# A hybrid encoder trunk on one core: two Strassen products moved between quarters, other preparation of the latents' weights

## The chip, the cores and the metric

The kernel runs on one core of a Trainium2 chip. The metric is the device time of one execution in microseconds, the median of several runs. The core has TensorE (matmuls, PE in the profile), VectorE (DVE), ScalarE (ACT), GpSimd (POOL) and SyncE (SP, which here only issues DMAs). Each engine works through its own instructions in order and waits on semaphores for the others.

## The reference

The input is a sequence of 512 tokens with 1024 channels, in float32, and everything stays float32 in effect. There are two layers, each a mixer and a feed-forward part, with an RMS norm before and after each:

```python
k_nope, k_rope, v = mla_shared_kv(h, ...)      # once, after layer 0
# layer 0's mixer: conformer_conv; layer 1's mixer: mla_attention on the shared K and V
h = h + rms_norm(m, mix_post_g[layer])
f = jnp.square(jax.nn.relu(rms_norm(h, ffn_pre_g[layer]) @ w_ff1[layer])) @ w_ff2[layer]
h = h + rms_norm(f, ffn_post_g[layer])
```

`mla_shared_kv` makes a latent of 256 for keys and values (`dkv`) with an RMS norm of its own, and a rotary key (`kr`). `mla_attention` makes a latent of 384 for the queries (`dq`), normalises it, and projects it to 8 heads of 128 plain and 64 rotary dimensions. Scores are scaled by 192 to the power −0.5, masked by chunks, and go through a softmax. The feed-forward part goes from 1024 to 4096 and back.

## The kernel before

**Splits.** A float32 matmul is made of three matmuls in a rounded type (`F32R`). Each operand is split into a high part (a ScalarE copy that rounds) and a low part (VectorE: operand minus high part), and the kernel adds high·high, high·low and low·high. Weights are split on the chip too: `weight(key)` loads a 128 x 1024 block into a `raw` tile and writes `wh` and `wl` tiles; there are 5 of each. For some blocks (`lo_by_dma`) ScalarE writes minus the high part instead, and an accumulating DMA of GpSimd's queue adds the weights. The latents' blocks `dq`, `dkv` and `kr` are first multiplied by a norm's gain, in eight GpSimd operations per block (`TENSOR_SCALAR raw<-raw,vt`), then split that way.

**Feed-forward.** `feed_forward(layer, X, F)` works in four quarters of the 4096 inner channels. In each, eight ff1 blocks of 24 matmuls give squared activations `Z`, and the second matrix is multiplied by Strassen's scheme over halves of tokens, of inner channels and of output columns: seven products of 24 matmuls. For each, `terms(p)` builds the left operand (a difference of two `Z` halves, then the split: four tiles per product), `weight` the right one (a sum or difference of blocks), and `collect` adds the two PSUM results to accumulators on VectorE. The order is `(3, 6, 2, 1, 4, 5, 7)` in quarters 0 to 2 and `(3, 5, 1, 4, 7, 2, 6)` in the last, so that there the first half of the tokens (blocks 0 and 1) is finished by products 5 and 7, and products 2 and 6 (`TOGETHER`) close the second half, one token block at a time. After the third quarter the accumulators are combined into the four output quadrants.

**Norm behind it.** `post_norm` takes the finished half rows. `residual` squares them (ScalarE, with a sum) and multiplies by the gain; `rms` and `rsqrt_tiny` make the scale in some ten VectorE operations of one or two columns (tiles `stat`), and `add_norm` adds the result to the residual `h`. In layer 0 it does so by halves of the tokens (`HA`, `HB`) and `prenorm` then transposes `h` on TensorE into 16 tiles `XH`. In layer 1 it does so by single blocks, with the gain's product on VectorE or GpSimd (`VG`), and each block is stored.

**Latents.** For each half, `latent("dq", ...)`, `latent("dkv", ...)` and the rotary key are made: products with `XH`, squares added, a sum over channels on TensorE, `rsqrt_tiny`, the scale spread over the partitions by four matmuls, then scaling, splitting and reordering. The projections of the first heads follow, and the attention, head by head: scores, `TENSOR_TENSOR_REDUCE` with the mask (it appears as `CUSTOM_DVE_ANT_0`), exponential with a sum on ScalarE, reciprocal and product on VectorE, transposes, and the product with the values.

**Tiles.** 50 tiles `big` of 128 x 512, 6 `tmp`, 6 `mm` and 2 `bc` in PSUM, and 8 `stat` serve everything.

**The order of work** is made by a planner in the program. It records all operations, gives each a due time from the recorded order of the matmuls, and plays the engines with costs (`cost`) and latencies; every engine takes the ready operation with the earliest due time, TensorE the one recorded first. DMAs are issued at most 16 us (`LEAD`) ahead. A `big` tile is given to an operation only when more tiles are free than tiles recorded earlier still wait for one. [...] Short matmuls with the identity (cost `FILL`) are put into planned gaps of TensorE. All instructions are issued through one helper, so the profile has them all on line 630, and one goes by tile names.

## Time and profile before

| | |
|---|---|
| median of 3 runs | 1086.79 us (1085.52 to 1087.72) |
| profiled execution, its own time | 1087.92 us |
| its span, first to last instruction | 1086.1 us |
| mean granted TensorE clock | 0.987 |
| HBM read, written | 197.58 MB, 5.51 MB |
| instructions | 15288 |

A name such as `wl<-raw,wh` is output from inputs. `mm<-big,wh` of 512 columns is an ff1 product or a projection, `mm<-wh,big` of 512 columns a Strassen product, `mm<-big,wh` of 256 columns a latent's product. A group's row has its count, its busy time and the mean time of one in ns, and then the idle time in front of it with what ended it. Consecutive instructions of one engine overlap in these records, so that an operation's duration is longer than the step from one to the next. The stages: convolution until about 205 us, layer 0's feed-forward until about 540, latents and attention until about 730, layer 1's feed-forward until 1069.7.

### The profile page before, as it was taken

The numbers are of one execution on the slowest core, as the hardware profiler recorded it, in microseconds if no ns is written. First come the engines' busy times: TensorE is split into PE (matmuls) and PEld (weight loads), VectorE is DVE, ScalarE is ACT, GpSimd is POOL, SyncE is SP. The second block draws the span as 40 slices with busy tenths as digits, with TensorE's granted clock in tenths as the row PEclk, the third lists the DMA queues.
The fourth block names the chain that finished last, engine by engine and source line by source line (L and its number), as shares of the span: only waits on it lengthen the run. The fifth ranks groups of instructions, "written<-read, shape, count | busy, mean of one in ns | idle before, by whom it ended". The sixth has DMA issues, their size and how long they took to land.

```text
span 1086.1 us, 15288 instructions
## 1 busy us (share of the span) xinstructions
PE 1046.9 (96%) x5310; PEld 889.3 (82%) x5310; DVE 762.1 (70%) x1523; ACT 643.5 (59%) x1364; POOL 191.1 (18%) x227
## 2 busy tenths in 40 slices
PE   9999989999999999999798999999999999999993
PEld 7888978988888888888687888889888888878883
DVE  6599973856458559848877977456663584588598
ACT  8563586956555455456775876568665644544561
POOL 1110011101001001002953443211010010010022
PEclk9999999999999999999899999999999999999997
DMA  8998687768958858839652133348596597588682
GB/s 271 315 282 222 206 232 194 175 162 241 236 144 239 237 143 238 259 122 265 158 138 74 50 97 120 135 157 210 153 256 201 153 245 216 156 216 228 197 213 78
DMA packets 67614, 207.25 MB, mean 191 GB/s; under 512 B 7632, under 2 KB 13904, under 8 KB 67536
## 3 DMA queue, kind: packets, MB, share of 16 engines
q1 hardware_dynamic: 48960, 150.16, 40.8%
q0 software_dynamic: 14400, 52.44, 26.7%
q10 hardware_dynamic: 4176, 3.67, 1.1%
q8 instruction: 42, 0.69, 0.3%
q14 instruction: 36, 0.29, 0.1%
HBM read 197.58 MB, written 5.51 MB: 187 GB/s over the span
## 4 chain that ended last, share of the span: by engine, by line
PE 78%; DVE 8%; DMA 6%; ACT 4%; issue 2%; POOL 2%; DVEq 0%; SPq 0%; POOLq 0%; ACTq 0%
PE mm L630 75%; DMA raw<-wts 4%; DVE big L630 4%; PE bc L630 3%; DVE wl L630 2%; ACT big L630 2%; DVE stat L630 2%; POOL raw L630 2%; ACT wh L630 1%; DMA wl<-raw 1%; DMA wl<-wts 1%; ACT wl L630 1%; DVE tmp L630 0%; DVE h L630 0%; DMA big<-xT 0%
## 5 line engine op out<-in xcount | busy, mean ns | idle before, releaser
L630 PE MATMUL mm<-big,wh 128*128 128x512 f32 (+1 forms) x1704 | 476.9, 364 | 2.0 <-ACT wh L630 0.8
L630 PE MATMUL mm<-wh,big 128*128 128x512 f32 (+1 forms) x1216 | 374.2, 387 | 5.7 <-ACT wh L630 2.9
L630 PEld LDWEIGHTS mm<-big,wh 128*128 128x128 f32 x1704 | 307.2, 190 | 52.6 <-DVE big L630 1.5
L630 ACT ACTIVATE wh<-raw 128x512 fp32r<-128x512 f32 (+2 forms) x456 | 258.8, 612 | 135.0 <-DMA raw<-wts 67.1
L630 DVE TENSOR_TENSOR wl<-raw,wh 128x512 fp32r<-128x512 f32 (+1 forms) x353 | 230.1, 689 | 145.0 <-ACT wh L630 144.5
L630 PE MATMUL mm<-big,wl 128*128 128x512 f32 (+1 forms) x852 | 309.4, 364 | 2.9 <-DMA wl<-raw 2.0
L630 PEld LDWEIGHTS mm<-wh,big 128*128 128x128 f32 x1216 | 227.1, 189 | 51.7 <-ACT wh L630 3.7
L630 PE MATMUL mm<-wl,big 128*128 128x512 f32 (+1 forms) x608 | 234.4, 387 | 2.6 <-DVE wl L630 2.6
L630 PEld LDWEIGHTS mm<-big,wl 128*128 128x128 f32 x852 | 161.4, 190 | 28.1 <-DMA wl<-raw 2.2
L630 POOL DMA_DIRECT2D raw<-wts x64 | 55.3, 864 | 557.2 <-DVE big L630 181.8
L630 PEld LDWEIGHTS mm<-wl,big 128*128 128x128 f32 x608 | 114.7, 189 | 27.4 <-DVE wl L630 5.0
L630 ACT ACTIVATE tmp<-mm 128x512 f32<-128x512 f32 (+1 forms) x72 | 39.8, 553 | 118.0 <-PE mm L630 118.0
L630 ACT ACTIVATE big<-tmp 128x256 f32<-128x256 f32 (+1 forms) x208 | 96.3, 494 | 21.1 <-DVE tmp L630 19.6
L630 DVE TENSOR_TENSOR big<-big,big 128x512 f32<-128x512 f32 (+5 forms) x101 | 69.5, 705 | 16.8 <-ACT big L630 16.1
L630 ACT ACTIVATE big<-mm 128x512 f32<-128x512 f32 (+5 forms) x110 | 57.5, 527 | 30.7 <-PE mm L630 29.9
L630 DVE TENSOR_TENSOR tmp<-big,big 128x512 f32<-128x512 f32 x80 | 53.7, 684 | 28.8 <-ACT big L630 28.7
L630 DVE TENSOR_TENSOR big<-big,mm 128x512 f32<-128x512 f32 x104 | 67.6, 677 | 4.6 <-PE mm L630 4.4
L630 DVE TENSOR_TENSOR big<-tmp,big 128x512 fp32r<-128x512 f32 (+1 forms) x93 | 59.7, 648 | 15.6 <-ACT big L630 13.6
L630 DVE SCALAR_TENSOR_TENSOR big<-big,vt,big 128x512 fp32r<-128x512 f32 (+20 forms) x95 | 63.2, 730 | 6.0 <-ACT big L630 6.0
L630 POOL DMA_DIRECT2D wl<-wts x30 | 26.5, 882 | 183.6 <-ACT wl L630 137.2
L630 ACT ACTIVATE wl<-raw 128x512 fp32r<-128x512 f32 x72 | 42.1, 623 | 13.2 <-POOL raw L630 6.1
L630 PE MATMUL mm<-big,big 128*128 128x512 f32 (+3 forms) x256 | 45.7, 325 | 0.0
(85 smaller groups left out, 810.9 us busy)
## 6 DMA issues: line engine op xcount, KB each, us to landing
raw<-wts SPq DMA_DIRECT2D x228, 512.0 KB, 5.1
raw<-wts POOLq DMA_DIRECT2D x64, 512.0 KB, 7.6
wl<-wts POOLq DMA_DIRECT2D x30, 512.0 KB, 8.4
big<-cw SPq DMA_DIRECT2D x45, 256.0 KB, 7.0
wl<-raw POOLq DMA_DIRECT2D x6, 512.0 KB, 5.2
row<-along SPq DMA_DIRECT2D x5, 512.0 KB, 4.5
raw<-wts SPq DMA_DIRECT2D x12, 192.0 KB, 2.4
big<-xT SPq DMA_DIRECT2D x8, 256.0 KB, 5.2
```

The source lines that it names most:

```text
L630: return f(*args, **kwargs)
```

## The change

- In both layers, products 2 and 6 of the third quarter are no longer made there. Their left operands are built at the end of that quarter and kept; the products are made in the fourth quarter behind product 7, into the PSUM tiles to which the fourth quarter's products 2 and 6 then add. Their four collecting sums go. The orders are now `(3, 6, 2, 1, 4, 5, 7)`, the same, `(3, 1, 4, 5, 7)` and `(3, 5, 1, 4, 7)`, the fourth followed by 2 and 6 of both quarters.
- The latents' blocks go into `big` tiles (`scaled`): two raw, two high and two low tiles per block, the gain by one VectorE product per 512 columns, the low part by VectorE. GpSimd's scalings and accumulating DMAs for them go.
- The queries' latent is not normalised. It is split straight from PSUM with `q_norm_g` as scale (`query_latent`), and the scale per query, together with 192 to the power −0.5, is kept in `wq` and applied in the softmax: one more VectorE operation per score tile, and a scale per row in the exponential. The order per half is now `dkv`, `kr`, `dq` 0 and 1; `dq` 2 is made once, for all tokens.
[...]
- The gain's product of the last norm stays on VectorE (`GAIN_ON`); `post_norm` takes its groups of blocks as an argument (`PAIRS`, `SINGLES`, `by_halves`), with the same groups as before.

The diff, cut to this:

```diff
-PRODUCTS = (3, 6, 2, 1, 4, 5, 7), (3, 5, 1, 4, 7, 2, 6)
+PRODUCTS = ((3, 6, 2, 1, 4, 5, 7),) * 2 + ((3, 1, 4, 5, 7), (3, 5, 1, 4, 7))
...
-        for p in PRODUCTS[q == 3]:
+        for r, p in [(q, p) for p in PRODUCTS[q]] + [(r, p) for r in (2, 3) for p in TOGETHER if q == 3]:
...
-FILL = 216.0
+FILL = 222.0
...
-            wide = [a for a in aps[1] if a.tensor.space != PSUM and _size(a) > 8]
+            wide = [a for a in aps[1] if a.tensor.space != PSUM]
...
+    def scaled(name, src):
+        lo, hi = ([big(F32R) for _ in range(2)] for _ in range(2))
+        for o in range(2):
+            raw = big()
+            nc.sync.dma_start(out=raw, in_=src[:, o * T : (o + 1) * T])
+            g0 = VEC[GAINS[name[0]]] + 4 * o
+            gain = vt[:, g0 : g0 + 4].rearrange("p (k o) -> p k o", o=1).to_broadcast([P, 4, P])
+            nc.vector.tensor_tensor(
+                out=raw.rearrange("p (k m) -> p k m", m=P), in0=raw.rearrange("p (k m) -> p k m", m=P), in1=gain, op=ALU.mult
+            )
+            split(raw, slice(0, T), (hi[o], lo[o]))
+        return hi, lo
...
-                    nc.gpsimd.tensor_scalar(
-                        out=raw[:, ks], in0=raw[:, ks], scalar1=v(GAINS[name[0]], k), scalar2=None, op0=ALU.mult
-                    )
...
+            steps = [(u, i) for u in range(2) for i in range(2)]
+            for p in PRODUCTS[q]:
+                A = terms(p)
+                collect(p, product({}, A, sides(q, p), steps))
...
+            if q > 1:
+                for p in TOGETHER:
+                    both[q, p] = terms(p)
             if q == 3:
-                both = {p: terms(p) for p in TOGETHER}
+                pts = {p: product({}, both[2, p], sides(2, p), steps, last=False) for p in TOGETHER}
+                w = {p: sides(3, p) for p in TOGETHER}
                 for i in range(2):
                     for p in TOGETHER:
-                        collect(p, product(*both[p], [(0, i), (1, i)]))
+                        product(pts[p], both[3, p], w[p], [(0, i), (1, i)], first=False)
+                        collect(p, {i: pts[p][i]})
                         yield done((1, int(p == 6)), i)
...
-            residual(F, g, b, dh, 16 + 2 * (b % nb) + dh, st[i], VG if nb == 1 else GAIN_ON, r2)
+            residual(F, g, b, dh, 16 + 2 * (b - bs[0]) + dh, st[bs], GAIN_ON, r2)
...
+    def query_latent(m, t):
+        t0, n = t
+        pt = products(("dq", m), XH, t0, n)
+        src, nat = dealt_part(pt[:, :n]), slice(t0, t0 + n)
+        hi, lo = (undealt(a, t) for a in CQ[m])
+        nc.scalar.activation(hi, src, AF.Copy, scale=v("q_g", m))
+        nc.vector.scalar_tensor_tensor(
+            out=lo, in0=src, scalar=v("q_g", m), in1=hi.bitcast(F32), op0=ALU.mult, op1=ALU.subtract
+        )
...
-        latent("dq", "q_g", CQ, t, 384)
...
+        for m in range(2):
+            query_latent(m, t)
+    query_latent(2, FULL)
...
+    nc.vector.tensor_copy(out=r, in_=sums([(b, r1n, b) for b in range(TB)], 0, D))
+    sm = sums([(b, qsq, b) for b in range(TB)], 0, 384)
...
+    nc.vector.scalar_tensor_tensor(out=wq, in0=y, scalar=8.0 * scale, in1=r, op0=ALU.mult, op1=ALU.mult)
...
-                out=S[:, ks], in0=sc[:, ks], in1=mask[:, T - nkey :], scale=-scale, scalar=-NEG,
-                op0=ALU.add, op1=ALU.min, accum_out=st[:, 0:1],
+                out=S[:, ks], in0=sc[:, ks], in1=mask[:, T - nkey :], scale=1.0, scalar=NEG,
+                op0=ALU.add, op1=ALU.max, accum_out=st[:, 0:1],
             )
-            nc.scalar.activation(S[:, ks], S[:, ks], AF.Exp, scale=-1.0, bias=st[:, 0:1], accum_out=st[:, 2:3])
+            w = wq[:, i : i + 1]
+            nc.vector.tensor_scalar(out=st[:, 1:2], in0=st[:, 0:1], scalar1=w, scalar2=-1.0, op0=ALU.mult, op1=ALU.mult)
+            nc.scalar.activation(S[:, ks], S[:, ks], AF.Exp, scale=w, bias=st[:, 1:2], accum_out=st[:, 2:3])
```

## The prediction

> **What bounds the kernel now.** I read the page first (sections 1, 2 and 4), then the windows around the two places that the change touches, then TensorE's waits and the timelines there.

> ```profile
> span 1086.1 us, 15288 instructions
> PE 1046.9 (96%) x5310; PEld 889.3 (82%) x5310; DVE 762.1 (70%) x1523; ACT 643.5 (59%) x1364; POOL 191.1 (18%) x227
> PE 78%; DVE 8%; DMA 6%; ACT 4%; issue 2%; POOL 2%; DVEq 0%; SPq 0%; POOLq 0%; ACTq 0%
> ```

> TensorE is the bound nearly everywhere, and the change takes away almost no matmul. So it can only fill stretches in which TensorE stands. Stage by stage (columns: window, length, busy PE, PEld, DVE, ACT, POOL, granted clock, DMA share, GB/s):

> ```profile
> 435.00:489.60 54.60, 54.60 (x243) 45.21 (x242) 36.24 (x60) 26.78 (x54) 2.59 (x3) 1.00 0.64 191
> 489.60:516.80 27.20, 27.20 (x122) 22.52 (x121) 23.95 (x40) 16.03 (x32) 8.80 (x13) 1.00 1.00 262
> 516.80:559.40 42.60, 34.73 (x201) 29.97 (x200) 33.31 (x90) 31.82 (x79) 37.87 (x52) 0.88 0.69 163
> 516.80:606.00 89.20, 78.45 (x507) 70.27 (x506) 68.94 (x186) 63.89 (x153) 54.10 (x69) 0.94 0.47 116
> 522.50:525.90 3.40, 2.92 (x9) 1.90 (x7) 3.40 (x6) 3.40 (x7) 2.48 (x3) 0.50 0.89 175
> 606.00:727.00 121.00, 119.36 (x667) 103.22 (x667) 81.04 (x208) 78.51 (x186) 40.13 (x34) 1.00 0.37 121
> 950.00:990.00 40.00, 38.51 (x168) 30.98 (x167) 35.75 (x61) 18.73 (x35) 3.45 (x4) 1.00 0.84 230
> 1031.30:1058.60 27.30, 27.30 (x122) 22.59 (x121) 26.37 (x45) 17.68 (x35) 6.68 (x6) 1.00 0.88 216
> 1058.60:1069.70 11.10, 11.07 (x49) 8.75 (x47) 11.03 (x24) 3.52 (x10) 2.54 (x2) 1.00 0.00 0
> 1069.70:1082.70 13.00, 0.00 (x0) 0.00 (x0) 12.97 (x42) 1.79 (x6) 3.94 (x3) 0.59 0.31 115
> ```

> A 512-column matmul costs 54.60/243 = 0.225 us, a Strassen product of 24 costs 5.4 us. Five products of layer 0's last quarter end at 516.8, and layer 1's at 1058.6. Two places are slack. From 516.8 to 606 (products 2 and 6, the latents, the first projections) TensorE is idle 89.20 − 78.45 = 10.7 us, and the clock is 0.12 × 42.6 = 5.1 us short in three half-rate stretches, one of which is shown: 15.8 us recoverable. And after the last matmul VectorE alone works for 13.0 us. What TensorE waits for from 516.8 to 606 (total, times, longest), and the worst case of it:

> ```profile
> PE mm L630 <- ACT wh L630: 2.9, 1, 2.9
> PE mm L630 <- DVE big L630: 2.5, 2, 2.3
> PE bc L630 <- DVE stat L630: 2.0, 2, 1.6
> PE mm L630 <- DMA wl<-raw: 2.0, 1, 2.0
> 534.24 0.63 ACT L630 ACTIVATE wl<-raw 128x512 fp32r<-128x512 f32 x1 [1.25 <-POOL raw L630]
> 535.39 1.13 ACT L630 ACTIVATE wh<-raw 128x512 fp32r<-128x512 f32 x2
> 536.05 1.19 PE L630 MATMUL mm<-wh,big 128*128 128x512 f32 x2 [2.90 <-ACT wh L630]
> L630 POOL TENSOR_SCALAR raw<-raw,vt 128x128 f32<-128x128 f32 x48 | 35.6, 972 | 2.3 <-DMA raw<-wts 2.3
> wl<-raw POOLq DMA_DIRECT2D x6, 512.0 KB, 5.2
> ```

> ScalarE runs in order. The latents' `wl<-raw` waits there for GpSimd's gain, and behind it stands the `wh<-raw` that product 6 needs. So GpSimd's 48 scalings (35.6 us) hold TensorE twice: through ScalarE, and through the accumulating DMA behind them (5.2 us). The 2.0 us for `stat` are the normalisations of the latents.

> **The change part by part.** Prices: VectorE's 128x512 operation repeats every (2.47 − 0.68)/3 = 0.60 us.

> ```profile
> 500.09 2.47 DVE L630 TENSOR_TENSOR big<-big,mm 128x512 f32<-128x512 f32 x4
> L630 DVE TENSOR_TENSOR wl<-raw,wh 128x512 fp32r<-128x512 f32 x5 | 3.2, 680 | 0.0
> L630 DVE SCALAR_TENSOR_TENSOR big<-big,vt,tmp 128x256 f32<-128x256 f32 x10 | 4.5, 478 | 2.8 <-ACT tmp L630 2.7
> L630 DVE TENSOR_TENSOR big<-big,big 128x256 fp32r<-128x256 f32 x10 | 7.0, 731 | 0.8 <-ACT big L630 0.7
> L630 DVE TENSOR_TENSOR big<-big,tmp 128x256 f32<-128x256 f32 x5 | 2.6, 529 | 0.9 <-ACT tmp L630 0.8
> 560.71 0.16 DVE L630 TENSOR_TENSOR stat<-bc,stat 128x2 f32<-128x2 f32 x1 [0.75 <-PE bc L630]
> 562.68 0.16 DVE L630 TENSOR_TENSOR stat<-stat,stat 128x2 f32<-128x2 f32 x1
> big<-cw SPq DMA_DIRECT2D x45, 256.0 KB, 7.0
> ```

> The chain of 11 small operations (first and last row) takes 562.84 − 560.71 = 2.1 us.

> *Latents' weights and the moved products, 516.8 to 606.* Removed: 48 GpSimd scalings, 12 ScalarE copies, 6 accumulating DMAs. Added on VectorE: per block two gain products and two low parts, 6 × 4 × 0.60 = 14.4 us; on SP, 12 loads of 256 KB in place of 6 of 512 KB, which now wait for big tiles. The queries' normalisation goes from the chain: 2 × (3 × 0.478 + 3 × 0.731 + 2 × 0.529 + 2.1) = 13.6 us of VectorE. In its place come four half and one full-width scaled low part (6 half widths × 0.73 = 4.4), squares added (4 half widths, 2.9), and one chain for `wq` (2.5): 9.8 us, off the path, because 39 matmuls of projections (8.8 us) stand ahead of the first softmax; without that cover the 2.5 us of the `wq` chain would be a wait. The postponed products bring eight low parts of weights into the quarter, 4.8 us, half of them ahead of 516.8. VectorE there: 68.9 + 14.4 − 13.6 + 9.8 + 2.4 = 82 us. TensorE: 78.45 − 5.1 of slow clock + 48 × 0.225 = 84.2 us, entered 10.8 us earlier. Perfectly packed this gains 15.8 us. VectorE at 97% would be as full as from 1031.3 to 1058.6 (26.37 of 27.30), where TensorE did not wait at all; from 516.8 on, though, norms in chains alternate with matmuls. Bounds: 0 (VectorE's order makes as many waits as GpSimd's did; below it lies the rival on tiles) and 15.8. I take 8, half: the waits by GpSimd (2.9 + 2.0), and half of clock and rest.

> The half-rate stretches follow waits of 2.0 to 2.9 us, and each costs 1.7 us. [...]

> *The tail of layer 1.* VectorE after 1058.6:

> ```profile
> L630 DVE SCALAR_TENSOR_TENSOR stat<-stat 128x1 f32<-128x1 f32 x20 | 5.8, 308 | 0.0
> L630 DVE TENSOR_TENSOR stat<-stat 128x1 f32<-128x1 f32 x12 | 2.6, 227 | 0.0
> L630 DVE SCALAR_TENSOR_TENSOR stat<-stat,r 128x1 f32<-128x1 f32 x4 | 1.7, 419 | 0.0
> L630 DVE TENSOR_SCALAR stat<-stat 128x1 int32<-128x1 int32 x4 | 0.6, 148 | 0.0
> L630 DVE SCALAR_TENSOR_TENSOR h<-big,stat,h 128x512 f32<-128x512 f32 x8 | 5.7, 744 | 0.0
> L630 POOL TENSOR_TENSOR big<-big,row 128x512 f32<-128x512 f32 x7 | 9.8, 1404 | 23.0 <-ACT tmp L630 23.0
> ```

> It works 11.03 + 12.97 = 24.0 us past product 7. Of that 20 × 0.16 + 12 × 0.08 + 4 × 0.27 = 5.2 us are stretched small operations (0.15 us is the undisturbed price), while GpSimd multiplies by the gain: five of its seven products fall here (x2 and x3 in the windows). In the changed kernel these five go to VectorE, 3.0 us, and the stretching goes; (2,6)'s low parts add 2.4 to 4.8. That is 24 to 27 us, against 2 × 5.4 + 11.1 = 21.9 us of matmuls behind product 7, so VectorE's backlog at the last matmul falls from 13 to about 2 to 5 us. Then the last block's own chain decides: collecting sum 0.7, square 0.6 like the ScalarE copies above, small chain 2.1, two sums 1.4, and signals between them: about 5.5. I put 8 us in place of 13: −5. Bounds: 0 and −7.5.

> [...]

> *Attention.* One more small VectorE operation per score tile, 32 in all, between maximum and exponential, and a scale from memory on the exponential.

> ```profile
> L630 DVE RECIPROCAL stat<-stat 128x1 f32<-128x1 f32 x32 | 4.9, 157 | 3.0 <-ACT big L630 2.8
> PE bc L630 <- DVE big L630: 1.1, 2, 0.8
> ```

> Priced as the reciprocal that it resembles, 4.9 us of VectorE at 67% load; from 606 to 727 TensorE waits 1.1 us for it. Bounds −0.5 and +5; I take +0.8, near the wait, since the next head's scores cover it.

> *Smaller parts.* The third quarter loses two products with their weights and four collecting sums, with less VectorE work per matmul; product 1, which subtracts weights, moves up to second place. The 950 to 990 window shows 1.5 us idle there; −1.5 to +2, taken as 0. The eight operand tiles kept until the fourth quarter take 8 of 50 big tiles; free ones while ff1 runs cover it. `dq` 2 at full width is 24 matmuls for 48 of half the width: 0. The planner's new costs reorder everything slightly: ±2, taken as 0.

> Sum: −8 − 5 + 0.8 = −12.2 us. The profiled execution took 1087.92 us (span 1086.1): 1087.9 − 12.2 = 1075.7. It stands 1.1 above the runs' median of 1086.79, from which the same sum gives 1074.6; I put 1075.

> **The rivals.**

> *Everything hidden.* Transition and tail both reach their bounds: 1087.9 − 15.8 − 7.5 + 0.8 = 1065. For it: VectorE's 97% without a wait from 1031.3. Against: the chains.

> *VectorE takes GpSimd's place.* It gets 24 more large operations where it is already busy 69 of 89 us, delays the second half's norm, and the transition gains nothing. 1087.9 − 5 + 0.8 = 1084. For it: the 2.5 us waits for `DVE big`.

> *Big tiles come too late (slower).* Six blocks need 24 big tiles and raw ones beside, while 8 results, 8 kept operands, 16 transposed residuals and 8 operands of the last products live: 40 of 50, before rope tables and masks. One block at a time, with 7.0 us for a load and 3 × 0.6 behind it, is ready every 8.8 us, but consumed in 24 × 0.225/2 = 2.7: 6.1 us of wait per block. SP is in order, so the projections' loads queue behind. Three such blocks cost 18.3, less the 6.6 of the waits (2.9 + 2.0) and the clock stretch (1.7) that they replace: 1087.9 + 11.7 − 5 = 1095. It decides from the second serial block. Against: the transposed tiles and freed operands come before 10.8 us of matmuls end.

> *It doesn't do what it says.* The moved weights fill VectorE as the old tail did, the transition waits for the residual's norms anyway: 1087.

> **How the numbers follow.** Forecast 0.50 (its own range 1067 to 1084), all hidden 0.13, VectorE instead 0.14, tiles late 0.13, nothing 0.10. A measurement here can tell about 0.2% (2.2 us). Faster: 0.50 + 0.13 + 0.14 = 0.77; same 0.08; slower 0.13 + 0.02. The range goes from 1064 (all hidden) to 1089, leaving out most of the tiles' case.

> **What would show it.** Right: idle TensorE between product 7 and the first scores falls from 10.7 to under 6 us with fewer half-rate stretches; no GpSimd scaling; VectorE ends within 8 us of the last matmul, small operations at 0.15 us. Wrong: `DMA raw<-wts` into big tiles or `DVE big` as TensorE's longest wait there, or an unchanged 13 us tail.

## The result, and the profile after

The changed kernel takes 1073.6 us in the median (1072.49 to 1075.48), the kernel before, beside it, 1087.26 us: a ratio of 0.9878 (0.9859 to 0.9897), or 13.7 us less. The forecast was 1075.0. The profiled execution took 1072.49 us. Its page, span, engines and chain:

```profile
span 1070.7 us, 15196 instructions
PE 1049.4 (98%) x5306; PEld 884.4 (83%) x5306; DVE 765.5 (71%) x1560; ACT 640.7 (60%) x1343; POOL 143.1 (13%) x165
PE 76%; DVE 12%; DMA 5%; ACT 5%; issue 1%; SPq 0%; ACTq 0%; DVEq 0%
big<-wts SPq DMA_DIRECT2D x12, 256.0 KB, 6.3
```

GpSimd has left the chain and lost 48 us of work (191.1 to 143.1), and VectorE has 3.4 us more of it in all. TensorE's busy time rose by 2.5 us though its mathematics is the same and 5.1 us of half clock went. Added identity matmuls (52 for 32, 8.1 us for 5.9) explain 2.2 us of this. The rest is the clue to what the prediction missed.

The windows of the kernel after, with the columns as before: from the end of product 7 to the first scores, then layer 1's last products and its tail. The fence ahead of them has the first of these stretches in the kernel before.

```profile
516.80:603.50 86.70, 75.95 (x495) 68.12 (x494) 66.50 (x178) 61.40 (x147) 53.67 (x69) 0.94 0.48 118
```

```profile
510.80:593.50 82.70, 82.01 (x530) 73.09 (x529) 75.06 (x181) 61.92 (x138) 23.20 (x23) 1.00 0.47 125
1010.70:1038.40 27.70, 27.70 (x122) 22.64 (x121) 26.29 (x44) 15.96 (x31) 3.45 (x4) 1.00 0.96 243
1038.40:1060.50 22.10, 22.10 (x97) 17.68 (x95) 21.62 (x56) 11.19 (x23) 1.72 (x2) 1.00 0.63 168
1060.50:1070.70 10.20, 0.00 (x0) 0.00 (x0) 6.95 (x25) 0.82 (x2) 0.00 (x0) 0.61 0.28 103
```

The stretch after product 7 now holds the two moved products (10.8 us of matmuls) and is still 4.0 us shorter. TensorE stands for 82.70 − 82.01 = 0.7 us in it where it stood for 10.75, at clock 1.00 in place of 0.94. What it still waits for there:

```profile
PE bc L630 <- DVE h L630: 0.4, 2, 0.2
PE mm L630 <- ACT big L630: 0.3, 1, 0.3
```

Not all of the old idle time has gone: the planner put 22 identity matmuls (2.5 us, at 544 us) into a gap that it foresaw, where the kernel before has 8. A planned gap shows as busy TensorE, so fillers are to be counted beside the waits. The groups of VectorE behind the last matmul:

```profile
L630 DVE SCALAR_TENSOR_TENSOR h<-big,stat,h 128x512 f32<-128x512 f32 x4 | 2.9, 744 | 0.0
L630 DVE TENSOR_TENSOR big<-big,row 128x512 f32<-128x512 f32 x4 | 2.7, 685 | 0.0
L630 DVE SCALAR_TENSOR_TENSOR stat<-stat 128x1 f32<-128x1 f32 x9 | 1.3, 154 | 0.1
L630 DVE SCALAR_TENSOR_TENSOR stat<-stat,r 128x1 f32<-128x1 f32 x2 | 0.3, 152 | 0.0
```

25 operations where 42 stood, the gain's products on VectorE, and small ones at 0.15 us: VectorE ends 7.2 us after the last matmul instead of 13.0.

Three marks cut the two executions at the same operations: the first and the last operation of the softmax's maximum on VectorE, and the last matmul. Before, then after:

```profile
603.54 0.29 DVE L630 CUSTOM_DVE_ANT_0 big<-mm,big 128x128 f32<-128x128 f32 x1
684.65 0.68 DVE L630 CUSTOM_DVE_ANT_0 big<-mm,big 128x512 f32<-128x512 f32 x1
1069.28 0.39 PE L630 MATMUL mm<-wh,big 128*128 128x512 f32 x1
```

```profile
593.51 0.28 DVE L630 CUSTOM_DVE_ANT_0 big<-mm,big 128x128 f32<-128x128 f32 x1
675.96 0.68 DVE L630 CUSTOM_DVE_ANT_0 big<-mm,big 128x512 f32<-128x512 f32 x1
1060.10 0.39 PE L630 MATMUL mm<-wh,big 128*128 128x512 f32 x1
```

| us, after minus before | predicted | measured | from |
|---|---|---|---|
| transition, product 7 to first scores | −8 | −14.8 | 82.7 − 86.7 − 10.8 moved in |
| all ahead of it | 0 | +4.8 | 510.8 − 516.8 + 10.8 moved out |
| attention | +0.8 | +1.3 | 82.45 − 81.11 |
| layer 1's feed-forward | 0 | −0.5 | 384.14 − 384.63 |
| tail | −5 | −6.2 | (1070.7 − 1060.1) − (1086.1 − 1069.28) |
| sum | −12.2 | −15.4 | spans 1070.7 and 1086.1 |

So two terms were too small and a loss of about 4 us, in stages that do the same work as before, was not in the sum. That loss is looked for first. The forecast for the tail was about the end of VectorE's work, which moved from 13.0 to 7.2 us behind the last matmul, −5.8.

The table rests on one execution of each kernel. A second profile of each (`r1_before`, `r1_after`, below) gives −18.0, +2.4, +1.4, +3.0 and −6.3 for the same rows. Attention and tail repeat within 0.1 us; the other rows scatter by 2 to 4 us. The loss, second and fourth row together, is there in both pairs: 4.3 and 5.4 us.

### The profile page after: what moved, and what is told of

Same layout as the page of the kernel before. It is cut to its first block, busy times and chain, and to the rows that moved or that the text cites. A ratio compares the mean times of both kernels' runs of the same rounds, so it can differ in the third digit from the quotient of the medians.

```text
span 1070.7 us, 15196 instructions
## 1 busy us (share of the span) xinstructions
PE 1049.4 (98%) x5306; PEld 884.4 (83%) x5306; DVE 765.5 (71%) x1560; ACT 640.7 (60%) x1343; POOL 143.1 (13%) x165
## 4 chain that ended last, share of the span: by engine, by line
PE 76%; DVE 12%; DMA 5%; ACT 5%; issue 1%; SPq 0%; ACTq 0%; DVEq 0%
PE mm L630 73%; DVE big L630 9%; DMA raw<-wts 3%; PE bc L630 2%; ACT big L630 2%; ACT wh L630 1%; DVE wl L630 1%; ACT wl L630 1%; DMA dealt<-big 1%; DVE stat L630 1%; DMA wl<-wts 1%; ACT tmp L630 1%; DVE h L630 1%; DVE tmp L630 1%; SPq L630 0%
## 5 line engine op out<-in xcount | busy, mean ns | idle before, releaser
L630 PE MATMUL mm<-big,wh 128*128 128x512 f32 (+1 forms) x1512 | 441.9, 374 | 1.4 <-ACT wh L630 1.0
L630 PE MATMUL mm<-wh,big 128*128 128x512 f32 (+1 forms) x1216 | 374.3, 387 | 0.2 <-ACT wh L630 0.2
L630 PEld LDWEIGHTS mm<-big,wh 128*128 128x128 f32 x1512 | 274.9, 188 | 55.1 <-ACT wh L630 2.5
L630 ACT ACTIVATE wh<-raw 128x512 fp32r<-128x512 f32 (+2 forms) x444 | 252.3, 612 | 110.6 <-PE mm L630 51.4
L630 DVE TENSOR_TENSOR wl<-raw,wh 128x512 fp32r<-128x512 f32 (+1 forms) x353 | 227.4, 683 | 125.8 <-ACT wh L630 119.8
L630 PE MATMUL mm<-big,wl 128*128 128x512 f32 (+1 forms) x756 | 282.1, 374 | 0.9 <-DMA wl<-wts 0.7
L630 PEld LDWEIGHTS mm<-wh,big 128*128 128x128 f32 x1216 | 226.0, 188 | 46.9 <-ACT wh L630 0.6
L630 PE MATMUL mm<-wl,big 128*128 128x512 f32 (+1 forms) x608 | 235.1, 387 | 0.2 <-DVE wl L630 0.2
L630 PEld LDWEIGHTS mm<-big,wl 128*128 128x128 f32 x756 | 141.9, 188 | 27.9 <-DVE wl L630 2.1
L630 PEld LDWEIGHTS mm<-wl,big 128*128 128x128 f32 x608 | 114.2, 188 | 24.0 <-DVE wl L630 0.8
L630 POOL DMA_DIRECT2D raw<-wts x64 | 55.5, 867 | 575.5 <-DMA raw<-wts 233.1
L630 ACT ACTIVATE big<-tmp 128x256 f32<-128x256 f32 (+1 forms) x208 | 96.8, 495 | 39.3 <-DVE tmp L630 37.5
L630 ACT ACTIVATE tmp<-mm 128x512 f32<-128x512 f32 (+1 forms) x75 | 42.2, 562 | 118.3 <-PE mm L630 117.6
L630 DVE TENSOR_TENSOR big<-big,big 128x512 f32<-128x512 f32 (+5 forms) x106 | 73.6, 708 | 38.8 <-ACT big L630 38.2
L630 PE MATMUL mm<-big,big 128*128 128x256 f32 (+3 forms) x520 | 83.4, 310 | 0.3 <-ACT big L630 0.3
L630 PEld LDWEIGHTS mm<-big,big 128*128 128x128 f32 x520 | 73.1, 190 | 5.8 <-ACT big L630 1.1
L630 ACT ACTIVATE big<-mm 128x512 f32<-128x512 f32 (+5 forms) x106 | 56.3, 535 | 28.4 <-PE mm L630 27.8
L630 DVE TENSOR_TENSOR big<-tmp,big 128x512 fp32r<-128x512 f32 (+1 forms) x95 | 60.9, 644 | 12.5 <-ACT big L630 10.7
L630 DVE TENSOR_TENSOR tmp<-big,big 128x512 f32<-128x512 f32 x80 | 54.1, 686 | 19.9 <-ACT big L630 19.8
L630 DVE SCALAR_TENSOR_TENSOR big<-big,vt,big 128x512 fp32r<-128x512 f32 (+29 forms) x95 | 63.0, 730 | 6.1 <-ACT big L630 6.1
L630 DVE TENSOR_TENSOR big<-big,mm 128x512 f32<-128x512 f32 x96 | 63.1, 681 | 3.1 <-PE mm L630 2.8
L630 POOL DMA_DIRECT2D wl<-wts x30 | 26.1, 870 | 181.4 <-ACT wl L630 157.6
## 6 DMA issues: line engine op xcount, KB each, us to landing
raw<-wts SPq DMA_DIRECT2D x222, 512.0 KB, 4.9
raw<-wts POOLq DMA_DIRECT2D x64, 512.0 KB, 7.8
wl<-wts POOLq DMA_DIRECT2D x30, 512.0 KB, 8.1
big<-cw SPq DMA_DIRECT2D x45, 256.0 KB, 5.9
big<-wts SPq DMA_DIRECT2D x12, 256.0 KB, 6.3
row<-along SPq DMA_DIRECT2D x5, 512.0 KB, 5.6
big<-xT SPq DMA_DIRECT2D x8, 256.0 KB, 4.8
```

The costliest lines, as they stand in the source:

```text
L630: return f(*args, **kwargs)
```

## Experiments: the loss in untouched stages

In a stretch of nothing but 512-column matmuls (ff1 blocks and Strassen products of layer 0), with TensorE never idle, 76 us hold 337 of them before and 334 after. From start to start that is 226.7 ns and, as a mean, about 229 ns. The rows are of before, after, and two experiments below (`r2_b_shift`, `r4_same_places`):

```profile
330.00:406.00 76.00, 76.00 (x337) 62.94 (x336) 49.65 (x82) 38.77 (x76) 6.92 (x8) 1.00 0.76 207
```

```profile
330.00:406.00 76.00, 76.00 (x334) 62.33 (x333) 48.13 (x79) 38.17 (x75) 6.90 (x8) 1.00 0.74 208
```

```profile
330.00:406.00 76.00, 76.00 (x333) 62.19 (x332) 49.16 (x80) 39.66 (x77) 6.92 (x8) 1.00 0.76 207
```

```profile
330.00:406.00 76.00, 76.00 (x337) 62.94 (x336) 49.30 (x81) 38.28 (x76) 6.91 (x8) 1.00 0.76 211
```

With 3702 such matmuls in the program, 2 ns each is some 7 us. First: is it the chip or the kernel? Both kernels unchanged, side by side on one chip.

> The kernel before, again, for its matmul step beside the changed kernel's on one chip. In the profile of the kernel before, a 512-column matmul followed the last by 226.7 ns, in that of the changed kernel by about 229 ns, in stages that the change does not touch. Theory C (the chip or the run): on one chip both show the same step, within 0.3 ns. Theory K (the kernel: other places of the tiles in memory, other neighbours): this one shows 226.7 and the changed one 229 again, which is some 8 us of the changed kernel's time.

> The changed kernel, again. Both theories: 12 to 15 us below the kernel before. Theory C: its step is that of the kernel before on this chip. Theory K: its step is 1% longer.

The kernel before had 337 matmuls in that window again (a single execution of 1090.96 us), the kernel after 334, at 1074.34 us against 1087.05, ratio 0.9882 (0.9864 to 0.99). The step belongs to the kernel.

What differs for those matmuls is where their operands lie. The change allocates the small tile `wq` (16 bytes per partition, which take 32), and all `big`, `raw`, `wh`, `wl` and `tmp` tiles but the first of each move by 32 bytes. Three runs move them otherwise, without touching the order of work:

```diff
 # r2_b_shift: the kernel before, 48 bytes more
-r2 = one(f"r2_{layer}", [P, TB])
+r2 = one(f"r2_{layer}", [P, TB + 12 * layer])
 # r2_al_after, r3_al128: the kernel after, tiles on other multiples
-wq, r1n = one("wq", [P, TB]), big()
+wq, r1n = one("wq", [P, 16])[:, :TB], big()   # r3_al128: 32
```

> The kernel before with one edit: a small tile (r2 of layer 1) is 16 columns wide instead of 4, which moves the same tiles by 32 bytes off the multiples of 64. The order of instructions is the same. Theory A: the step rises from 226.7 to about 229 ns, the time by 7 to 9 us, to 1095. Rival: no change, 1087.

> The changed kernel with one edit: the tile wq is 16 columns wide instead of 4 (64 bytes instead of 32 in memory), of which 4 are used. The order of instructions is the same on every engine; all big, raw, wh, wl and tmp tiles but the first of each move by 32 bytes, back to multiples of 64, where the kernel before has them. Theory A (the 32-byte offset that wq brought slows every matmul): the 512-column step falls from about 229 to 226.7 ns, some 4000 such steps by 2.3 ns are 9 us: 1064 to 1066. Rival (the step depends on the order of work or the neighbours, not on the places): no change, 1074.

> The changed kernel with the tile wq 32 columns wide (128 bytes in memory), 4 of them used. The order of instructions is the same. The places of the big, wh and wl tiles, but the first of each, are multiples of 128 again, as in the kernel before; with 64 bytes they were at 64 beyond such a multiple, with 32 at 32. Steps so far: 226.7 ns at 0, about 229 at 32, 228 to 229 at 64. Theory A128 (the step is shortest at multiples of 128): 226.7 ns, 1064 to 1067, the fastest so far. Rival (only the kernel before's own places are good, or the order matters beside the place): 228 ns or more, 1072 to 1075.

`r2_b_shift`: 1094.78 us against 1088.82, ratio 1.0063 (1.0039 to 1.0086), with 333 matmuls in the window (row above). The kernel before, made slower by 6.0 us by nothing but the tiles' places: that places matter is shown. But the two rules that I tried for which places are good both fell. With tiles on 64 modulo 128 the kernel after took 1073.6 us, ratio 0.9867 (0.9845 to 0.9889), and on multiples of 128 it took 1073.81, 0.9877 (0.9849 to 0.9905), both still with 334 in the window. So I stopped guessing a modulus and put every tile exactly where the kernel before has it, with `wq` in spare columns of an existing small tile:

```diff
+small.append(one(f"r2_{layer}", [P, (2 - layer) * TB]))
+r2 = small[layer][:, :TB]
...
-wq, r1n = one("wq", [P, TB]), big()
+wq, r1n = small[0][:, TB:], big()
```

> The changed kernel with wq kept in four spare columns of the tile r2 of layer 0, in place of a tile of its own. The order of instructions is the same; every tile stands exactly where it stands in the kernel before. Theory P (the places alone set the matmul's step, and those of the kernel before happen to be good): the step is 226.7 ns in all stages without other work, and about 4200 full-width steps' worth of time by 2 ns or somewhat more come off: 1063 to 1067, the fastest of all. Rival (the changed order or its neighbours make the step long, and in the kernel before with shifted places it was something else): 228 ns or more, 1072 to 1075.

1068.42 us (1067.33 to 1069.66) against 1088.99: ratio 0.9818 (0.9788 to 0.9849), the best of all kernels here, 5 to 6 us under the change as made (1073.6 us, and 1074.34 on this chip), and 337 matmuls in the window. It came out 1.4 us above the expected range. In its profile, part of what the quicker matmuls gave came back: TensorE waits 2.4 us in layer 1's feed-forward, where the change as made waits 1.2, and a half-rate stretch of the convolution is longer: from 147 us on, 12 matmuls `bc<-col` take 2.60 us there in place of 1.79. Its marks:

```profile
590.54 0.28 DVE L630 CUSTOM_DVE_ANT_0 big<-mm,big 128x128 f32<-128x128 f32 x1
672.96 0.68 DVE L630 CUSTOM_DVE_ANT_0 big<-mm,big 128x512 f32<-128x512 f32 x1
1056.36 0.39 PE L630 MATMUL mm<-wh,big 128*128 128x512 f32 x1
```

The first scores come 13.0 us earlier than before, where the change as made has 10.0. Attention (82.42) is as in the change as made, so its 1.3 us are not the places.

The steps do not lengthen evenly. The 229 ns are a mean. Between 330 and 406 us all 335 steps of the kernel before are 226 or 227 ns; of the kernel after's 332 steps 119 are 229 to 236 ns, in runs of up to 17 matmuls, and the others 224 to 228. The first tile of each name kept its address when all others moved by 32 bytes. So where a matmul reads a first tile and a moved one, as its two operands, their start addresses are no longer a multiple of 512 bytes apart. In the kernel after this holds for 756 of the 3702 matmuls of 512 columns, in the kernel before for 2 of 3678, in `r4_same_places` for 2. In the profile of the kernel after, such matmuls take 233.1 ns in the mean (743 steps under 245 ns, 725 of them 229 or more) and the others 228.2 (2894 steps, 802 of them 229 or more); in that of the kernel before the mean is 227.1. Against this mean the first lose 4.5 us together and the others 3.3. So more than half of the lengthening lies in such pairs, and moving nearly all tiles by 32, 64 or 128 bytes made 754 to 784 of them each time (`r2_al_after`, `r3_al128`, `r2_b_shift`). No run moved a single tile, so that the distance lengthens the step was not shown; what lengthens the other steps is open.

## Experiments: which part earns what

**The gain's product, alone.** The kernel before with the last norm's gain on VectorE.

```diff
-residual(F, g, b, dh, ..., st[i], VG if nb == 1 else GAIN_ON, r2)
+residual(F, g, b, dh, ..., st[i], GAIN_ON, r2)
```

> The kernel before with one edit: the last norm's gain product stays on VectorE. Theory 1 (GpSimd's five late products stretch VectorE's small operations by 5.2 us; five products of 0.6 come instead): the tail behind the last matmul falls from 13.0 to about 11 us, the time by 2 us, 1085. Rival (only the cover of the moved matmuls shortens the tail): within 0.5 us of the kernel before.

1088.67 against 1087.05, ratio 1.0016 (0.9998 to 1.0034): nothing gained. Its tail, window and two groups of VectorE:

```profile
1070.70:1086.70 16.00, 0.00 (x0) 0.00 (x0) 12.24 (x40) 2.44 (x6) 0.00 (x0) 0.58 0.35 131
```

```profile
L630 DVE SCALAR_TENSOR_TENSOR stat<-stat 128x1 f32<-128x1 f32 x12 | 1.7, 152 | 0.0
L630 DVE TENSOR_TENSOR big<-big,row 128x512 f32<-128x512 f32 x5 | 3.4, 682 | 0.0
```

In the kernel before, behind the last matmul:

```profile
L630 DVE SCALAR_TENSOR_TENSOR stat<-stat 128x1 f32<-128x1 f32 x16 | 4.2, 287 | 0.0
```

The small operations fall from 287 to 152 ns, as the prediction had it. But of the 5.2 us of stretching that it counted only 16 × 0.135 + 4 × 0.267 = 3.2 us lay behind the last matmul, and four more gain products there take 2.7 us of that. From last matmul to end, the tail is 16.4 us for 16.9. The theory that the stretching costs the tail 2 us fell, and its rival is nearer, though the time came out 1.6 us above the kernel before and not within 0.5. What shortens the tail is matmuls to work behind.

**The moved products: without them, and alone.** `r1_a_nodefer` is the kernel after with products 2 and 6 back in the third quarter, `r3_b_defer` the kernel before with them moved (the diff of the change's `PRODUCTS` and `both`, alone).

```diff
 # r1_a_nodefer
-PRODUCTS = ((3, 6, 2, 1, 4, 5, 7),) * 2 + ((3, 1, 4, 5, 7), (3, 5, 1, 4, 7))
+PRODUCTS = ((3, 6, 2, 1, 4, 5, 7),) * 3 + ((3, 5, 1, 4, 7),)
...
-pts = {p: product({}, both[2, p], sides(2, p), steps, last=False) for p in TOGETHER}
+pts = {p: {} for p in TOGETHER}
```

> The changed kernel with products 2 and 6 of the third quarter back in the third quarter, all else as changed. Theory 1 (the moved matmuls cover VectorE's work at both ends of the last quarter): the tail grows by 3 to 4 us, and TensorE waits 3 to 8 us between layer 0's last products and the latents; 1080 to 1086. Rival (the latents' weights off GpSimd are all of the gain): within 2 us of the changed kernel.

> The kernel before with the moved products alone (places as before). Theory S (each part helps by itself): the tail shortens by 4 to 6 us, the transition somewhat, 1078 to 1081. Theory N (the parts need each other: GpSimd's scalings then still hold the latents, whatever covers): only the tail gains, and some of it is lost to VectorE; 1082 to 1088.

`r1_a_nodefer`: 1090.89, ratio 1.0035 (1.002 to 1.0049), 16.5 us above the kernel after on the same chip and well beyond what I expected. Its windows from 510 us to the first scores and behind the last matmul, and the groups of identity matmuls:

```profile
510.00:605.10 95.10, 90.50 (x581) 79.97 (x580) 84.81 (x194) 63.89 (x141) 25.84 (x26) 1.00 0.39 108
1071.60:1086.70 15.10, 0.01 (x1) 0.00 (x0) 12.04 (x40) 2.44 (x6) 0.00 (x0) 0.58 0.37 139
```

```profile
L630 PE MATMUL mm<-ident 128*128 128x128 f32 x40 | 6.4, 323 | 1.5 <-POOL big L630 1.5
L630 PE MATMUL bc<-ident 128*128 128x128 f32 x50 | 6.3, 281 | 0.0
```

The tail is nearly the old one, 4.9 us longer than after. The first scores come 11.7 us later than in the kernel after (605.18 for 593.51), and most of that is seen in the transition: 4.6 us of idle TensorE (95.10 − 90.50) for 0.7, and 90 fillers where the kernel after has 52, some 4 us. Without the two products' 10.8 us, the norms have too little to hide behind.

`r3_b_defer`: 1087.41 against 1089.2, ratio 0.9986 (0.9964 to 1.0008). Two windows, in the transition and behind the last matmul, and TensorE's longest waits from 500 to 610 us:

```profile
546.00:556.00 10.00, 5.55 (x42) 4.90 (x43) 6.73 (x20) 7.18 (x21) 10.00 (x17) 1.00 0.82 163
1075.30:1087.40 12.10, 0.00 (x0) 0.00 (x0) 7.97 (x26) 0.95 (x4) 1.26 (x1) 0.68 0.29 108
```

```profile
PE mm L630 <- ACT wh L630: 4.4, 5, 1.6
PE bc L630 <- DVE h L630: 3.5, 3, 2.3
PE bc L630 <- DVE stat L630: 2.3, 3, 1.1
```

The tail is over 4 us shorter, but the postponed work meets GpSimd's scalings in the transition, where GpSimd is busy without a break (10.00 us of 10) and TensorE for 5.55. So the transition gains nothing: the first scores come at 608.0 us, where the two profiles of the kernel before have 603.5 and 607.9. Layer 1's feed-forward takes 386.6 us, 2 to 3 more than in these two, with a half-rate stretch of 3.4 us (1.7 lost) and 2.2 us of waiting for a weight's DMA; which of the two stages takes more of what the tail gains is within this scatter. Theory N held: only the tail gains, and the time is not clear of the kernel before's.

**The latents' weights: alone, and GpSimd's way put back.** `r3_b_weights` is the kernel before with `scaled` alone; `r2_al_gpsw` is the kernel after (with the places of `r2_al_after`) with GpSimd's scalings and `lo_by_dma` for the latents.

> The kernel before with the latents' weights in big tiles and VectorE's gain alone (places as before, normalised queries, order of products as before). Theory S: the waits by GpSimd go, 5 to 8 us: 1079 to 1082. Theory N (without the moved products VectorE has no room for 14.4 us more in that stretch, as the 16 us of the changed kernel without the moved products say): 1085 to 1092.

> The changed kernel with aligned tiles and the latents' weights prepared as before (GpSimd's gain in the raw, wh and wl tiles, accumulating DMA), all else as changed. Theory 1 (GpSimd's 48 scalings hold TensorE through ScalarE's order and the DMA): 5 to 10 us above the aligned changed kernel, TensorE idle again between layer 0's products and the latents. Rival (the moved products alone cover them): within 2 us.

Alone: 1085.48 against 1089.2, ratio 0.9977 (0.9961 to 0.9993), 3.7 us. The waits for GpSimd go, but the planner sees others coming and fills them, with 104 identity matmuls where the kernel before has 32:

```profile
L630 PE MATMUL mm<-ident 128*128 128x128 f32 x48 | 7.8, 315 | 1.5 <-POOL big L630 1.5
L630 PE MATMUL bc<-ident 128*128 128x128 f32 x56 | 7.3, 280 | 0.0
```

Put back: 1086.18 against 1088.82, ratio 0.9981 (0.9962 to 0.9999), so 12.6 us above `r2_al_after`, more than the 5 to 10 expected. The transition's waits are led by the one that the prediction named, ScalarE's `wh` behind GpSimd's gain, and two half-rate stretches of 3.4 us are back in it (1.7 us lost in each):

```profile
PE mm L630 <- ACT wh L630: 7.2, 5, 3.3
PE bc L630 <- DVE stat L630: 0.3, 1, 0.3
```

**The queries' latent, normalised again.** `r2_a_norm` is the kernel after with `latent("dq", ...)` per half and the old softmax; it has no `wq`, and so the places of the kernel before.

> The changed kernel with the queries' latent normalised as before (no wq, no added operation per score tile), all else as changed. Its tiles stand at multiples of 64. Theory 1: the normalisations' waits come back, 1 to 3 us, less 0.8 in the attention: 1 to 3 us above the changed kernel with aligned tiles, 1065 to 1069. Rival (the unnormalised queries cost in the attention what they gain): within 1 us of the aligned changed kernel.

1078.32 against 1088.82, ratio 0.9908 (0.9886 to 0.9931), far above the 1065 to 1069 expected. By the kernel with the same places (0.9818, on another chip), the unnormalised queries are worth about 10 us, or 6 to 14 by the two intervals; `dq` 2 made once instead of per half is a part of that. TensorE's waits from 500 to 700 us:

```profile
PE bc L630 <- DVE big L630: 5.2, 6, 1.4
PE mm L630 <- DVE big L630: 3.2, 5, 1.2
PE mm L630 <- DVE wl L630: 2.3, 2, 1.2
```

Together: moved products −1.8 (not clear of noise) and weights −3.7 alone; both of them, with the gain and the planner's costs, −10.5 (`r2_a_norm`); with the queries as well −20.6 (`r4_same_places`). Taking one of the three out costs 16.5, 12.6 and about 10 us. So the values do not add. As the waits and fillers above read, the parts share one resource, the cover of the transition, and each alone only shows the next wait.

## Why the prediction was right

*What bounds the kernel, and where the slack lies:* right. TensorE's idle time and clock from product 7 to the first scores, and the tail, gave all of the gain; nothing else did.

*The transition term was mis-sized.* I took half of the 15.8 us because chains of norms alternate with matmuls, and because VectorE would be at 97%. The parts that I named for it, all of GpSimd's waits and half of clock and rest, add up to 4.9 + 5.4 = 10.3 us and not to 8. Measured, 14.8 us came (with the old places, where product 7 ends at about 507.4, 86.7 + 10.8 − 83.1 = 14.4), near the bound, and VectorE was at 75.06 of 82.70, 91%. The chains were covered by what I had counted only as work moved: 10.8 us of matmuls that wait for nothing in the transition. `r1_a_nodefer` shows it: without them 4.6 us stand idle again. The queries' chain off the path, which I counted as 13.6 us of VectorE less 9.8, is worth about 10 us by `r2_a_norm`, as its waits for VectorE's `big` and `wl` show.

*The clock:* the half-rate stretches there went with the waits, 5.1 us, as the sum had it. That they follow waits of 2.0 to 2.9 us is not the whole of it: in `r3_b_defer` TensorE waits 2.3 us for `h`, and the window from 546 us around it keeps clock 1.00. Length alone does not decide, then. In the profile of the kernel before, the half-rate stretches begin at 143.59, 522.47, 536.12, 549.77 and, behind the last matmul, 1072.01 us, which are 111, 4, 4 and 153 times 3.413 us apart; in that of the kernel after at 144.51 and 1062.69 us, 269 times. In windows of this length, counted from these starts, TensorE was busy for 0.51 to 1.41 us of the 3.41 ahead of all seven; all other windows up to the last matmul have 1.83 us or more, and none of those at full clock was followed by half rate. Two neighbouring windows of the kernel before, then two pairs of `r3_b_defer`, the first with the wait for `h`:

```profile
546.36:549.77 3.41, 1.41 (x12) 1.21 (x12) 3.41 (x11) 2.40 (x8) 3.41 (x6) 1.00 1.07 258
549.77:553.18 3.41, 3.41 (x19) 3.41 (x18) 1.49 (x5) 1.67 (x4) 3.41 (x8) 0.50 0.49 121
```

```profile
547.03:550.44 3.41, 2.07 (x16) 1.79 (x17) 3.31 (x5) 2.01 (x6) 3.41 (x7) 1.00 0.38 73
550.44:553.85 3.41, 2.13 (x19) 1.96 (x18) 1.64 (x5) 3.25 (x12) 3.41 (x8) 1.00 1.09 211
748.46:751.87 3.41, 1.17 (x10) 0.97 (x9) 2.94 (x8) 3.41 (x10) 0.00 (x0) 1.00 0.68 241
751.87:755.28 3.41, 3.41 (x18) 3.41 (x17) 0.66 (x2) 0.24 (x1) 1.72 (x2) 0.50 0.51 94
```

*The tail:* −6.2 (−5.8 for VectorE's end) for −5, for the right reason in the main. That the gain's place on VectorE pays was the weak link: `r1_b_gain` shows no gain from it. The cover of matmuls behind product 7 does it.

*Attention:* +1.3 for +0.8, but not as priced. TensorE's waits between the first and the last scores are 1.6 us before (1.1 and 0.5) and 1.0 after (0.8 and 0.2), so the added operation per tile is hidden. TensorE is busier instead, because the two marks do not hold the same matmuls. Before, after, and `r1_a_nodefer`:

```profile
603.50:684.65 81.15, 79.51 (x481) 70.39 (x480) 65.41 (x181) 60.93 (x150) 32.10 (x29) 1.00 0.28 86
```

```profile
593.50:675.95 82.45, 81.16 (x487) 71.50 (x486) 67.89 (x214) 64.21 (x151) 33.33 (x30) 1.00 0.27 83
```

```profile
605.15:684.90 79.75, 78.14 (x472) 68.70 (x471) 66.00 (x209) 61.12 (x146) 31.38 (x28) 1.00 0.24 75
```

The new order puts six more matmuls between the marks, two of 512 columns and five of 384 more and one of 128 less; by the 226.7 ns of a 512-column step these are, as an estimate, the 1.3 us. `r1_a_nodefer`, with the same softmax, has fewer and takes 79.75 us. So the term is about zero, and the 1.3 us are work that other stages no longer have.

*Third quarter, planner, `dq` 2, taken as 0:* with the old places what lies ahead of the transition is 507.4 − 516.8 + 10.8 = +1.4 us and layer 1's feed-forward 383.40 − 384.63 = −1.2, together about zero, so the terms hold as far as one profile of each can tell; no run has the planner's costs alone. *The step that failed* is that stages whose work is unchanged keep their price: the change's 16 bytes moved the tiles and cost 5 to 6 us (1073.6 and 1074.34 against 1068.42).

*The rivals:* "everything hidden" (1065) comes nearest to what the mechanism does, in both places: the kernel with the old places reaches 1068.4. "VectorE takes GpSimd's place" did not come: no wait for `DVE big` is left in the transition. Nor did "big tiles come too late": the 12 loads land in 6.3 us in the median and TensorE never waits for one. The forecast of 1075 thus owes its nearness to luck, to two errors of opposite sign: about 8 us too little gain, less some 5 us of unforeseen loss.

## What to carry to other kernels

Parts that draw on the same cover are to be priced together: here three parts whose single values are small lose 10 to 17 us when any one is missing. In a kernel with planned fillers, count the fillers with the waits, since a foreseen gap looks like busy TensorE. And when a new tile is added, compare the matmul step in a stage that the change doesn't touch, and try small tiles where they move nothing: here that was worth 5 to 6 us (`r4_same_places`).

## What was unexpected of the hardware

The step of back-to-back 512-column matmuls changed with the places of the SBUF tiles: 226.7 ns with those of the kernel before (330 to 406 us), 228.9 ns in the mean in the kernel after, where nearly all tiles stand 32 bytes further, and hardly better on 64 modulo 128 or on multiples of 128 (334 matmuls in the 76 us in all three, 337 before). In a kernel with 3678 of them this was 6.0 us of 1089 (`r2_b_shift`). In the kernel after, matmuls whose two operands do not start a multiple of 512 bytes apart take 233.1 ns in the mean and the others 228.2. What lengthens the steps was not shown.
